# Six edits to a decoder block: pool placement, PSUM banks kept, down loads reordered, pooling sums on GpSimd, priorities, a layer norm issued later

## The chip, the cores and the metric

The kernel runs on one core of one Trainium2 chip. The metric is the device time of one execution in microseconds (us), lower is better. TensorE (PE) multiplies matrices into PSUM; VectorE (DVE), ScalarE (ACT) and GpSimd (POOL) do the rest; nearly all DMA transfers are issued by SyncE (SP).

## The reference

One decoder block over 2048 tokens of width 1024, all in float32:

```python
mod = silu(c) @ w_ada + b_ada                 # sh1, sc1, g1, sh2, sc2, g2
h = layer_norm(x) * (1 + sc1) + sh1
a_val, a_gate, u_pool, gate_a, gate_b = split(h @ w_in)    # 512, 512, 512, 1024, 1024
ya = silu(layer_norm(causal_dwconv(a_val * sigmoid(a_gate), w_dw_a))) @ w_pw_a   # 31 taps
pooled = causal_means(u_pool, windows 2, 4, 8, 16 for 128 channels each) - u_pool
yb = (pooled @ w_pool, per group) * pool_scale
mix = (sigmoid(gate_a) * ya + sigmoid(gate_b) * yb) @ w_out
x = layer_norm(ALPHA * x + g1 * mix) * ln1_g + ln1_b
h = layer_norm(x) * (1 + sc2) + sh2
v, gt = split(causal_dwconv(h @ w_up, w_dw_f))             # 3 taps, 2 x 2816 channels
x = layer_norm(ALPHA * x + g2 * ((gelu(gt) * v) @ w_down)) * ln2_g + ln2_b
```

## The kernel before

Every product runs as three matmuls on two-part operands: `split` (L203, L204) rounds a tile to a high part on ACT and takes the low part by a subtraction on DVE, or on POOL for most weights (`lo_eng`). Operands live in 128 x 512 slots: 16 of pool `hp` (name `h`), 28 of `gp` (name `g`), and later 12 named `ex`. Weight tiles are `whi` and `wlo`, 128 x 1024, in pool `ws`, four of each.

The first part runs over four passes (`q`) of 512 tokens. A pass holds: the gated products (L239 to L241) and the start of the 31-tap convolution (taps on DVE, L527); for `q` > 0 the output projection of the pass before (`project`, L488 to L490); four pooling products, each followed by the sums of a causal window; eight gate products and pool products (`evacuate`, L438, multiplies a PSUM tile by scale and gate on DVE); the norm of the convolution branch; and `merge`, which multiplies and adds into `ms` (L454, L455) and splits the result. A sum over a window of `w` tokens is made by doubling: 1, 2, 3 and 4 adds (L567) for windows of 2, 4, 8 and 16, ten in a pass, each from one buffer `us` to the next; then L570 divides and subtracts `u`, in the first pass L572 and L573 mend the first columns, and `split` gives the operands.

The kernel uses eight PSUM banks of 128 x 512. Two are `ps_tr` for transposes throughout. In the first part four are `ps_mm` and two `ps_cv` (the convolution's start); both pools belong to the stack `s1`, which is closed after the fourth pass, and a pool `ps_mm2` of six banks is opened behind it.

The last projection, `project(3, ...)`, runs behind that point, with steps of `operands` between its matmuls: these make the 28 operand tiles of the up product. Its end is the first layer norm, four row tiles: statistics, a power on POOL (L258), ACT's scaling, four DVE operations each (L506, L507) and a store to `x1_dram`. Steps of `operands` reuse slots that the projection's matmuls release.

The up product runs over two halves of 1024 tokens (`hf`), 22 units each (`u`). A unit is one step of Strassen's scheme, seven products of `multiply` (L793 to L795); the weights come from `UpWeights`, whose sums run on POOL (L714). In the first half a generator `task`, advanced at four places of a unit from the second unit on, makes the second half's operands (`h2_store`). The results go to `f_dram`. In the second half `down_operands` stores the down weights' seven combinations (`dh_...`, `dl_...`) to DRAM.

The down product (L813 to L815) runs Strassen's seven combinations (`STEPS`) over 11 k tiles, two k tiles for each pair of weight loads (L947). `Gated.fetch` (L848) loads tiles of `f`, 256 KB each; a weight load is 512 KB. In step `s3` of the first half the operand of k tile `k` is made of `f[0][k]` and `f[1][k]` by L918. The loads of k tiles 0 to 7 are issued in the last unit of the up product, those of 8 to 10 ahead of the first weights, and during `s3` two tiles of `f[1][11...]` behind each weight pair, for the next step.

The order on each engine is made by the tile framework's scheduler, which places instructions by priority (program order, unless `high_priority` or `issue_after` says otherwise) and its own estimate of times. Each engine then runs its queue in that order, waiting on semaphores. SP's queue holds loads and stores alike; in it a transfer waits for one that was issued eight transfers earlier.

## Time and profile before

| | us |
|---|---|
| median of 3 runs | 2321.76 |
| lowest and highest | 2320.23, 2323.77 |
| the profiled execution | 2322.59 |
| its span | 2320.7 |

The profile's page gives busy time by engine, the list of waits says for whom an engine stood idle and how long, a table of windows gives busy times and the granted clock of TensorE for stretches of the span, and a timeline gives instructions one after the other. Times in a timeline start with the span. A matmul's duration in a row is longer than its turn on the engine, since matmuls overlap; the pace is read from the starts, 0.23 us apart at full clock. PEclk is the granted clock as a share of the higher of its two levels (2.4 GHz; the lower is 1.2).

### The profile page before, as it was taken

Reading aid. Unit: us, or ns where it says so; the run is one execution under the profiler, and the core shown is the slowest. Engines: PE = TensorE matmul, PEld = TensorE weight load, DVE = VectorE, ACT = ScalarE, POOL = GpSimd, SP = SyncE. Lnnn points to the kernel's source line nnn. Section 1 sums busy time; section 2 is a strip of 40 time slices with the busy share of each in tenths; the row PEclk is TensorE's granted clock in tenths of the full one; section 3 lists DMA queues with packets and bytes.
Section 4 is the critical chain, followed back from the end, with each engine's and each line's share of the span. In section 5 each row is a group of like instructions: output and inputs, shape, how many; then the busy total and the mean of one; then the engine's idle time right before and its main releaser. Section 6 shows DMA issues by size and latency. Waiting matters only on the chain.

```text
span 2320.7 us, 28743 instructions
## 1 busy us (share of the span) xinstructions
PE 2246.5 (97%) x9889; PEld 1834.1 (79%) x9889; DVE 1783.0 (77%) x2769; ACT 795.4 (34%) x1213; POOL 541.5 (23%) x428
## 2 busy tenths in 40 slices
PE   5999999999999999989999999999999989999997
PEld 4777887888887888768888888888888868887885
DVE  7996779476967695798899988877777774487467
ACT  3434121321232033246555445433333332333222
POOL 0543230000110010046555564522231300000000
PEclk9999999999999999999999999999999999999998
DMA  9988877585676577779999885999999997598665
GB/s 330 346 272 295 286 266 274 200 308 199 254 294 245 189 274 262 287 259 334 341 343 349 304 321 196 345 375 339 367 345 369 363 355 267 191 355 299 243 213 195
DMA packets 293227, 675.85 MB, mean 291 GB/s; under 512 B 24249, under 2 KB 113077, under 8 KB 293082
## 3 DMA queue, kind: packets, MB, share of 16 engines
q1 hardware_dynamic: 293082, 674.02, 80.3%
q8 instruction: 78, 1.28, 0.2%
q14 instruction: 67, 0.55, 0.1%
HBM read 460.53 MB, written 213.39 MB: 290 GB/s over the span
## 4 chain that ended last, share of the span: by engine, by line
PE 88%; DVE 5%; DMA 4%; issue 1%; ACT 1%; POOL 1%; SPq 1%; DVEq 0%; POOLq 0%; ACTq 0%
PE mm L793 11%; PE mm L795 11%; PE mm L794 11%; PE mm L239 9%; PE mm L241 9%; PE mm L240 9%; PE mm L813 6%; PE mm L815 6%; PE mm L814 6%; PE mm L488 2%; PE mm L489 2%; PE mm L490 2%; PE tr L278 1%; DMA g<-in_w_ada_dram 1%; DMA raw<-in_w_ada_dram 1%
## 5 line engine op out<-in xcount | busy, mean ns | idle before, releaser
L239 PE MATMUL mm<-h,whi 128*128 128x512 f32 x896 | 354.5, 398 | 5.9 <-DVE g L438 2.3
L240 PE MATMUL mm<-h,whi 128*128 128x512 f32 x896 | 351.9, 393 | 0.2 <-DVE h L204 0.2
L241 PE MATMUL mm<-h,wlo 128*128 128x512 f32 x896 | 351.6, 393 | 0.0
L527 DVE SCALAR_TENSOR_TENSOR cv<-y,wa,cv 128x512 f32<-128x512 f32 x464 | 318.6, 749 | 3.2 <-ACT cv L519 1.8
L804 DVE SCALAR_TENSOR_TENSOR o<-mm,wf,o 128x511 f32<-128x511 f32 (+2 forms) x352 | 257.5, 743 | 39.1 <-ACT o L800 34.7
L813 PE MATMUL mm<-whi,ex 128*128 128x512 f32 x616 | 241.0, 398 | 9.4 <-DMA whi<-dh_t 9.4
L814 PE MATMUL mm<-wlo,ex 128*128 128x512 f32 x616 | 243.9, 396 | 0.0
L815 PE MATMUL mm<-whi,ex 128*128 128x512 f32 x616 | 241.6, 396 | 0.0
L204 POOL TENSOR_TENSOR wlo<-raw,whi 128x512 fp32r<-128x512 f32 (+1 forms) x109 | 197.0, 1820 | 190.9 <-ACT whi L203 143.7
L800 ACT ACTIVATE o<-mm,par,wf 128x512 f32<-128x512 f32 x176 | 136.8, 779 | 304.7 <-DVE mm L889 183.5
L793 PE MATMUL mm<-g,whi 128*128 128x512 f32 x616 | 240.4, 391 | 0.7 <-DMA g<-xh_t 0.7
L794 PE MATMUL mm<-g,whi 128*128 128x512 f32 x616 | 241.1, 391 | 0.0
L795 PE MATMUL mm<-g,wlo 128*128 128x512 f32 x616 | 235.4, 390 | 0.0
L239 PEld LDWEIGHTS mm<-h,whi 128*128 128x128 f32 x896 | 169.5, 189 | 45.1 <-DVE g L438 2.8
L240 PEld LDWEIGHTS mm<-h,whi 128*128 128x128 f32 x896 | 169.8, 190 | 36.6 <-issue 1.6
L241 PEld LDWEIGHTS mm<-h,wlo 128*128 128x128 f32 x896 | 169.3, 189 | 35.6 <-issue 0.2
L258 POOL TENSOR_TENSOR rs<-ve,mhalf 128x1 f32<-128x1 f32 x64 | 40.8, 652 | 627.3 <-DVE ve L256 460.6
L813 PEld LDWEIGHTS mm<-whi,ex 128*128 128x128 f32 x616 | 116.2, 189 | 38.1 <-ACT ex L203 9.8
L793 PE MATMUL mm<-h,whi 128*128 128x512 f32 x352 | 138.6, 394 | 3.2 <-ACT whi L203 3.2
L795 PE MATMUL mm<-h,wlo 128*128 128x512 f32 x352 | 138.4, 393 | 1.7 <-DVE wlo L204 1.7
L794 PE MATMUL mm<-h,whi 128*128 128x512 f32 x352 | 138.4, 393 | 0.0
L815 PEld LDWEIGHTS mm<-whi,ex 128*128 128x128 f32 x616 | 115.9, 188 | 28.4 <-DVE ex L204 0.4
(223 smaller groups left out, 4311.9 us busy)
## 6 DMA issues: line engine op xcount, KB each, us to landing
whi<-hi_in SPq DMA_DIRECT2D x84, 512.0 KB, 4.5
wlo<-lo_in SPq DMA_DIRECT2D x84, 512.0 KB, 4.4
uh<-whi SPq DMA_DIRECT2D x70, 512.0 KB, 4.5
ul<-wlo SPq DMA_DIRECT2D x70, 512.0 KB, 4.8
whi<-uh SPq DMA_DIRECT2D x70, 512.0 KB, 5.3
wlo<-ul SPq DMA_DIRECT2D x70, 512.0 KB, 7.8
raw<-in_w_up_dram SPq DMA_DIRECT2D x48, 512.0 KB, 7.2
f<-o SPq DMA_DIRECT2D x44, 512.0 KB, 4.5
```

The costliest lines, as they stand in the source:

```text
L204: return (lo_eng or nc.vector).tensor_sub(lo, src, hi)
L239: nc.tensor.matmul(ps, lhsT=whi[k][:, ms], rhs=xhi, start=(k == 0), stop=False)
L240: nc.tensor.matmul(ps, lhsT=whi[k][:, ms], rhs=xlo, start=False, stop=False)
L241: nc.tensor.matmul(ps, lhsT=wlo[k][:, ms], rhs=xhi, start=False, stop=(k == n - 1))
L527: nc.vector.scalar_tensor_tensor(dst, ys[j][:, k:k + T], wa[:, j, k:k + 1], o, ALU.mult, ALU.add)
L793: nc.tensor.matmul(ps, lhsT=whi[:, k, :], rhs=xhi, start=(k == 0), stop=False)
L794: nc.tensor.matmul(ps, lhsT=whi[:, k, :], rhs=xlo, start=False, stop=False)
L795: nc.tensor.matmul(ps, lhsT=wlo[:, k, :], rhs=xhi, start=False, stop=(k == len(xs) - 1))
L804: nc.vector.scalar_tensor_tensor(dst, y[:, :n], wf[:, tap, t:t + 1], dst, ALU.mult, ALU.add)
L813: nc.tensor.matmul(ps, lhsT=fhi[:, tk], rhs=whi, start=(k == 0), stop=False)
L814: nc.tensor.matmul(ps, lhsT=fhi[:, tk], rhs=wlo, start=False, stop=False)
L815: nc.tensor.matmul(ps, lhsT=flo[:, tk], rhs=whi, start=False, stop=(k == NK - 1))
```

## The change

Six edits. (1) The pools `xp` and `sm` are placed at the other end of SBUF (`side="right"`), and an unused tile `pad` with its memset goes. (2) `ps_mm` and `ps_cv` belong to the kernel's own stack and are kept after the fourth pass; `psum()` then takes banks from both by a fixed turn, two of `ps_cv`, four of `ps_mm`. (3) In the last pass the merge's operations behind a matmul, and the projection's evacuation in every pass, get high priority. (4) The pooling sums run on GpSimd. (5) The last layer norm of the first part becomes a generator, which `task` runs through ahead of `h2_store`, and `task` is advanced in the first unit as well. (6) Of the first down loads those of k tiles 0 to 4 are issued ahead of the first weights, the rest two k tiles behind each weight pair of `s3`, and from the third pair on three tiles `f[1][11...]` behind each.

```diff
-    xp = ctx.enter_context(tc.tile_pool(name="xp", bufs=5))
-    sm = ctx.enter_context(tc.tile_pool(name="sm", bufs=6))
+    xp = ctx.enter_context(tc.tile_pool(name="xp", bufs=5, side="right"))
+    sm = ctx.enter_context(tc.tile_pool(name="sm", bufs=6, side="right"))
...
-    pad = sm.tile([P, 16], F32, name="pad", tag="pad", bufs=1)
-    nc.vector.memset(pad, 0.0)
+    turns = None
     def psum():
+        if turns is not None and next(turns):
+            return ps_cv.tile([P, T], F32, name="cv", tag="cv")
         return ps_mm.tile([P, T], F32, name="mm", tag="mm")
...
-    ps_mm = s1.enter_context(tc.tile_pool(name="ps_mm", bufs=4, space=bass.MemoryType.PSUM))
-    ps_cv = s1.enter_context(tc.tile_pool(name="ps_cv", bufs=2, space=bass.MemoryType.PSUM))
+    ps_mm = ctx.enter_context(tc.tile_pool(name="ps_mm", bufs=4, space=bass.MemoryType.PSUM))
+    ps_cv = ctx.enter_context(tc.tile_pool(name="ps_cv", bufs=2, space=bass.MemoryType.PSUM))
...
-            nc.vector.tensor_mul(sga[j], pa, sga[j])
-            nc.vector.tensor_add(ms[j], ms[j], sga[j])
-            hi, lo = slot(F32R), slot(F32R)
-            split(hi, lo, ms[j])
+            with tc.high_priority() if q == NQ - 1 else nullcontext():
+                nc.vector.tensor_mul(sga[j], pa, sga[j])
+                nc.vector.tensor_add(ms[j], ms[j], sga[j])
+                hi, lo = slot(F32R), slot(F32R)
+                split(hi, lo, ms[j])
...
-            for i in range(T // P):
-                nc.vector.scalar_tensor_tensor(zs[i][:, cl], zs[i][:, cl], ALPHA, po[i], ALU.mult, ALU.add)
+            with tc.high_priority():
+                for i in range(T // P):
+                    nc.vector.scalar_tensor_tensor(zs[i][:, cl], zs[i][:, cl], ALPHA, po[i], ALU.mult, ALU.add)
...
+        def norm():
+            for i in range(T // P):
+                z = zs[i]
+                normalise(z)
...
+                nc.sync.dma_start(x1_dram[q * (T // P) + i], z)
+                yield
+        return norm()
...
-            project(q - 1, mg)
+            for _ in project(q - 1, mg):
+                pass
...
-                nc.vector.tensor_add(nxt[:, a:], cur[:, a:], cur[:, a - d:15 + T - d])
+                nc.gpsimd.tensor_add(nxt[:, a:], cur[:, a:], cur[:, a - d:15 + T - d])
...
-    ps_mm = ctx.enter_context(tc.tile_pool(name="ps_mm2", bufs=6, space=bass.MemoryType.PSUM))
+    turns = cycle((True, True, False, False, False, False))
...
-        task = chain(h2_store(2), h2_store(3)) if hf == 0 else None
+        task = chain(last_norm, h2_store(2), h2_store(3)) if hf == 0 else None
...
-                if u and name in ("x11", "t2", "t3", "t4"):
+                if name in ("x11", "t2", "t3", "t4"):
...
-                gated.fetch((0, 1), range(8))
+                gated.fetch((0, 1), range(5))
...
-        if hf == 0:
-            gated.fetch((0, 1), range(8, NK))
+        rest = iter(range(5, NK)) if hf == 0 else iter(())
+        ahead = iter(range(NK, NF))
...
-                        gated.fetch((1,), [NK + kk for kk in ks])
+                        gated.fetch((0, 1), [kk for _, kk in zip(ks, rest)])
+                        if k >= 4:
+                            gated.fetch((1,), list(islice(ahead, 3)))
```

What the scheduler makes of it is shown at three places. In these rows a line stands first, then the operation, the output, `<-` and the inputs with buffer numbers, and what the instruction waits for. Line numbers after the change are 2 to 9 higher.

The first place is DVE in the first pass, from the last taps of the pooling stretch to the first evacuation (`us` are pooling sums, `cv` the convolution). Before:

```order
L567 TENSOR_TENSOR us_999<-us_997 128x512 [waits DVE_49]
L527 SCALAR_TENSOR_TENSOR cv_586<-y_582,wa_106,cv_586 128x512 [waits DVE_49]
L527 SCALAR_TENSOR_TENSOR cv_645<-y_641,wa_106,cv_645 128x512 [waits DVE_49]
L570 SCALAR_TENSOR_TENSOR us_1001<-us_999,u_989 128x512 [waits DVE_49]
L527 SCALAR_TENSOR_TENSOR cv_586<-y_582,wa_106,cv_586 128x512 [waits DVE_49]
L527 SCALAR_TENSOR_TENSOR cv_645<-y_641,wa_106,cv_645 128x512 [waits DVE_49]
L572 TENSOR_TENSOR us_1001<-us_999,rcnt_89 128x15 [waits DVE_49]
L573 TENSOR_TENSOR us_1001<-us_1001,u_989 128x15 [waits DVE_49]
L204 TENSOR_TENSOR g_1006<-us_1001,g_1005 128x512 [waits Activation_49]
L438 SCALAR_TENSOR_TENSOR g_1186<-mm_1182,par_105,sg_1180 128x512 [waits PE_49]
```

The same stretch of DVE after the change:

```order
L535 SCALAR_TENSOR_TENSOR cv_584<-y_580,wa_104,cv_584 128x512 [waits DVE_49]
L535 SCALAR_TENSOR_TENSOR cv_643<-y_639,wa_104,cv_643 128x512 [waits DVE_49]
L579 SCALAR_TENSOR_TENSOR us_999<-us_997,u_987 128x512 [waits Pool_49]
L581 TENSOR_TENSOR us_999<-us_997,rcnt_87 128x15 [waits DVE_49]
L582 TENSOR_TENSOR us_999<-us_999,u_987 128x15 [waits DVE_49]
L206 TENSOR_TENSOR g_1004<-us_999,g_1003 128x512 [waits Activation_49]
L440 SCALAR_TENSOR_TENSOR g_1184<-mm_1180,par_103,sg_1178 128x512 [waits PE_49]
```

And POOL there after the change, with the last four adds (`wlo` are weights):

```order
L206 TENSOR_TENSOR wlo_1231<-raw_1232,whi_1230 128x1024 [waits DMAHW3_49,DMAHW7_49,PE_49,Activation_49]
L570 COPY uh_798<-u_987 128x15 [waits Activation_49]
L576 TENSOR_TENSOR us_991<-u_987 128x526 [waits Pool_49]
L568 COPY u_2885<-uh_798 128x15 [waits DVE_49]
L576 TENSOR_TENSOR us_993<-us_991 128x524 [waits Pool_49]
L206 TENSOR_TENSOR wlo_1274<-raw_1275,whi_1273 128x1024 [waits DMAHW5_49,DMAHW6_49,PE_49,Activation_49]
L576 TENSOR_TENSOR us_995<-us_993 128x520 [waits DVE_49,Pool_49]
L576 TENSOR_TENSOR us_997<-us_995 128x512 [waits Pool_49]
L206 TENSOR_TENSOR wlo_1317<-raw_1318,whi_1316 128x1024 [waits DMAHW0_49,DMAHW1_49,PE_49,Activation_49]
```

The adds left DVE and stand between POOL's weight subtractions; the last subtraction of the pooling (L570, now L579) waits for POOL, the taps between it and L573 have moved ahead, and the evacuation L438 (now L440) follows it directly.

The second place is TensorE from the last merge product (L239 to L241) to the last projection's first matmuls. Before:

```order
L241 MATMUL mm_7846<-g_7631,wlo_7824 128x512
L488 MATMUL mm_7884<-whi_7888,g_7716 128x512 [waits DMAHW4_49,DVE_49,Activation_49]
L489 MATMUL mm_7884<-wlo_7889,g_7716 128x512 [waits DMAHW5_49]
L490 MATMUL mm_7884<-whi_7888,g_7717 128x512
L488 MATMUL mm_7885<-whi_7888,g_7716 128x512
```

After:

```order
L243 MATMUL mm_7844<-g_7629,wlo_7822 128x512
L491 MATMUL cv_7877<-whi_7881,g_7714 128x512 [waits DMAHW4_49,Activation_49]
L492 MATMUL cv_7877<-wlo_7882,g_7714 128x512 [waits DMAHW5_49]
L493 MATMUL cv_7877<-whi_7881,g_7715 128x512
L491 MATMUL cv_7878<-whi_7881,g_7714 128x512
L492 MATMUL cv_7878<-wlo_7882,g_7714 128x512
L493 MATMUL cv_7878<-whi_7881,g_7715 128x512
L491 MATMUL mm_7879<-whi_7881,g_7714 128x512 [waits DVE_49]
```

The first two accumulators are banks of `ps_cv` now, without a wait for DVE; the third and fourth are banks of `ps_mm` and wait for DVE.

The third place is SP's queue at the start of the down product (`h` and `g` are tiles of `f`, `dh_t3` and `dl_t3` the stored weights). Before, with four loads of `f` left out of the print ahead of it:

```order
L848 DMA h_16062<-f0_4_8388 128x512 [waits DMAHW7_49,PE_49]
L848 DMA h_16063<-f0_5_8389 128x512 [waits DMAHW0_49,PE_49]
L848 DMA h_16064<-f0_5_8389 128x512 [waits DMAHW1_49,PE_49]
L848 DMA h_16065<-f0_6_8390 128x512 [waits DMAHW2_49,PE_49]
L848 DMA h_16066<-f0_6_8390 128x512 [waits DMAHW3_49,PE_49]
L848 DMA h_16067<-f0_7_8391 128x512 [waits DMAHW4_49,PE_49]
L848 DMA h_16068<-f0_7_8391 128x512 [waits DMAHW5_49,PE_49]
```

Then come six loads of `f` for the k tiles 8 to 10, and behind them:

```order
L947 DMA whi_16202<-dh_t3_8436 128x1024 [waits DMAHW4_49]
L947 DMA wlo_16203<-dl_t3_8437 128x1024 [waits DMAHW5_49]
L848 DMA g_16206<-f0_11_8395 128x512 [waits DMAHW6_49,PE_49]
L848 DMA g_16207<-f0_12_8396 128x512 [waits DMAHW7_49,PE_49]
L947 DMA whi_16246<-dh_t3_8436 128x1024 [waits DMAHW0_49]
```

After:

```order
L857 DMA h_16055<-f0_4_8317 128x512 [waits DMAHW7_49,PE_49]
L956 DMA whi_16171<-dh_t3_8365 128x1024 [waits DMAHW0_49]
L956 DMA wlo_16172<-dl_t3_8366 128x1024 [waits DMAHW1_49]
L857 DMA h_16175<-f0_5_8318 128x512 [waits DMAHW2_49,PE_49]
L857 DMA h_16176<-f0_5_8318 128x512 [waits DMAHW3_49,PE_49]
L857 DMA h_16177<-f0_6_8319 128x512 [waits DMAHW4_49,PE_49]
L857 DMA h_16178<-f0_6_8319 128x512 [waits DMAHW5_49,PE_49]
L956 DMA whi_16219<-dh_t3_8365 128x1024 [waits DMAHW6_49,PE_49]
L956 DMA wlo_16220<-dl_t3_8366 128x1024 [waits DMAHW7_49,PE_49]
```

The first weight pair follows ten loads of `f` instead of 22, and four more loads stand between it and the second pair. Between the second and third pair stand four loads as well; between the third and the fourth four loads, three stores of weights of the last `down_operands`, and three loads of `f[1][11...]`; between the fourth and fifth one such store, three loads and the store of the last unit's result (512 KB).

## Rows read from the trace of the kernel before

**Rows 1.** Page, busy us, share of the span and instructions of each engine.

```profile
PE 2246.5 (97%) x9889; PEld 1834.1 (79%) x9889; DVE 1783.0 (77%) x2769; ACT 795.4 (34%) x1213; POOL 541.5 (23%) x428
```

**Rows 2.** TensorE's waits: line, releaser, us in total, times, longest.

```profile
PE mm L813 <- DMA whi<-dh_t: 9.4, 1, 9.4
...
PE mm L239 <- DVE g L438: 5.7, 2, 3.3
...
PE mm L488 <- ACT g L203: 3.7, 1, 3.7
...
PE mm L793 <- ACT ht L878: 2.6, 1, 2.6
PE mm L795 <- DVE wlo L204: 2.2, 2, 1.7
```

**Rows 3.** Windows: length, PE, PEld, DVE, ACT, POOL busy, PEclk, DMA share, GB/s.

```profile
120.00:136.00 16.00, 13.65 (x54) 10.82 (x54) 15.28 (x24) 4.75 (x7) 6.55 (x4) 0.89 0.84 280
945.00:957.00 12.00, 8.31 (x31) 6.49 (x30) 11.78 (x20) 4.81 (x8) 0.00 (x0) 0.86 0.85 320
960.00:990.00 30.00, 30.00 (x134) 24.86 (x133) 15.23 (x24) 4.07 (x7) 0.00 (x0) 1.00 0.65 234
```

**Rows 4.** Timelines, first pass: start, us, engine, line, operation, [idle before <-releaser].

```profile
110.49 2.51 POOL L204 TENSOR_TENSOR wlo<-raw,whi 128x1024 fp32r<-128x1024 f32 x1 [1.46 <-ACT whi L203]
...
110.66 1.41 DVE L527 SCALAR_TENSOR_TENSOR cv<-y,wa,cv 128x512 f32<-128x512 f32 x2
111.97 1.58 DVE L570 SCALAR_TENSOR_TENSOR us<-us,u 128x512 f32<-128x512 f32 x1
...
117.51 1.05 ACT L203 CAST whi<-raw 128x1024 fp32r<-128x1024 f32 x1
...
125.97 0.18 DVE L573 TENSOR_TENSOR us<-us,u 128x15 f32<-128x15 f32 x1
126.83 0.69 DVE L204 TENSOR_TENSOR g<-us,g 128x512 fp32r<-128x512 f32 x1 [0.68 <-ACT g L203]
127.44 0.74 DVE L438 SCALAR_TENSOR_TENSOR g<-mm,par,sg 128x512 f32<-128x512 f32 x1
...
128.23 0.80 PE L239 MATMUL mm<-h,whi 128*128 128x512 f32 x1 [2.35 <-DVE g L438]
```

**Rows 5.** Lines L567, L714: count, ns min/median/max, first and last start.

```profile
L567 DVE TENSOR_TENSOR us<-us x24: 636/680/2574, 103.4 to 843.4; 128x512 f32<-128x512 f32 x12, 128x516 f32<-128x516 f32 x4, 128x524 f32<-128x524 f32 x4, 128x520 f32<-128x520 f32 x4
L567 DVE TENSOR_TENSOR us<-u x16: 681/692/2496, 91.9 to 836.6; 128x512 f32<-128x512 f32 x4, 128x514 f32<-128x514 f32 x4, 128x518 f32<-128x518 f32 x4, 128x526 f32<-128x526 f32 x4
...
L714 POOL TENSOR_TENSOR st<-raw x24: 1284/1300/2361, 1000.0 to 1453.6; 128x512 f32<-128x512 f32 x24
```

**Rows 6.** Timelines, second pass: POOL, DVE and TensorE.

```profile
337.98 10.37 POOL L561 COPY uh<-u 128x15 f32<-128x15 f32 x2 [2.21 <-ACT u L560]
...
376.59 1.28 DVE L179 SCALAR_TENSOR_TENSOR xt<-raw,silu_c,xt 128x1024 f32<-128x1024 f32 x1 [0.34 <-DMA raw<-in_w_ada_dram]
...
378.40 2.06 DVE L438 SCALAR_TENSOR_TENSOR g<-mm,par,sg 128x512 f32<-128x512 f32 x3
...
379.19 0.50 PE L239 MATMUL mm<-g,whi 128*128 128x512 f32 x1 [3.35 <-DVE g L438]
```

**Rows 7.** Timelines, DVE and TensorE at the start of the last projection.

```profile
950.26 0.69 DVE L454 TENSOR_TENSOR g<-mm,g 128x512 f32<-128x512 f32 x1
...
951.05 0.77 PE L488 MATMUL mm<-whi,g 128*128 128x512 f32 x1 [3.69 <-ACT g L203]
```

**Rows 8.** Timelines, SP and TensorE at the down start, and a window behind it.

```profile
1856.73 4.45 SPq L848 DMA_DIRECT2D h<-f  x7
...
1866.00 0.32 SPq L947 DMA_DIRECT2D whi<-dh_t  x1
...
1872.11 2.05 PE L813 MATMUL mm<-whi,ex 128*128 128x512 f32 x4 [9.39 <-DMA whi<-dh_t]
...
1880.00:1890.00 10.00, 10.00 (x44) 8.04 (x44) 6.86 (x11) 1.38 (x3) 0.00 (x0) 1.00 1.04 412
```

More of the change, by code (lines that the diff above doesn't have):

```diff
@@ L1 @@
-from contextlib import ExitStack
-from itertools import chain
+from contextlib import ExitStack, nullcontext
+from itertools import chain, cycle, islice
 import concourse.bass as bass
@@ L500, in project @@
                 nc.sync.dma_start(gb[2 * i + hh], v[:, hh * T:(hh + 1) * T].broadcast_to([P, T]))
-        for i in range(T // P):
-            z = zs[i]
-            normalise(z)
-            for hh in range(2):
-                cl = slice(hh * T, (hh + 1) * T)
-                nc.vector.tensor_mul(z[:, cl], z[:, cl], gb[hh])
-                nc.vector.tensor_add(z[:, cl], z[:, cl], gb[2 + hh])
-            nc.sync.dma_start(x1_dram[q * (T // P) + i], z)
+        def norm():
+            for i in range(T // P):
+                z = zs[i]
+                normalise(z)
+                for hh in range(2):
+                    cl = slice(hh * T, (hh + 1) * T)
+                    nc.vector.tensor_mul(z[:, cl], z[:, cl], gb[hh])
+                    nc.vector.tensor_add(z[:, cl], z[:, cl], gb[2 + hh])
+                nc.sync.dma_start(x1_dram[q * (T // P) + i], z)
+                yield
+        return norm()
     yh = uh = None
@@ L692, in decoder_block @@
     gb = [t[:, hh * T:(hh + 1) * T] for t in (otile(), otile()) for hh in range(2)]
-    project(NQ - 1, mg, gb, {(0, 0): 1, (0, 1): 1, (0, 2): 1, (0, 3): 1, (0, 4): 1, (0, 5): 1, (0, 6): 1, (0, 7): 1,
+    last_norm = project(NQ - 1, mg, gb, {(0, 0): 1, (0, 1): 1, (0, 2): 1, (0, 3): 1, (0, 4): 1, (0, 5): 1, (0, 6): 1, (0, 7): 1,
                              (1, 0): 1, (1, 2): 1, (1, 5): 1, (1, 7): 1})
```

## Prediction

> **What bounds the kernel now.** I read the page's line of busy times, then TensorE's waits, then the stretches in which the larger waits lie. TensorE is busy for 2246.5 us of a span of 2320.7 us [rows 1], so only about 74 us of its time are idle, and no other engine's total matters by itself: an edit is worth what it takes out of these 74 us, plus what the clock loses behind a stall. The list of waits [rows 2] names five single events that the change touches: 9.4 us before the first matmul of the down product (a load of `whi`), 2.35 + 3.35 us before matmuls that wait for the evacuation at L438, 3.7 us at the start of the last output projection (L488), and 2.6 and 1.7 us in the first unit of the up product. The other events it leaves alone. The windows around the events [rows 3] show the second price: after a stop of 2.35 us and more the granted clock stands at the lower of its two levels for a few us. Over the 16 us around 128 us the mean is 0.89, which is 0.11 x 16 = 1.8 us lost; 0.14 x 12 = 1.7 us around 951 us. At 379 and 1872 us, behind stops as long or longer, I charge the same, 1.8 and 1.7 us. So the events cost: 128 us, 2.35 + 1.8 = 4.1; 379 us, 3.35 + 1.8 = 5.1; 951 us, 3.7 + 1.7 = 5.4; 1872 us, 9.4 + 1.7 = 11.1. Together 25.7 us are within reach.
>
> **Pooling sums on GpSimd.** DVE loses 40 adds of about 0.68 us, ten in each of the four passes [rows 5], and POOL gains them. A POOL operation of the same kind and size (L714) has a median of 1.30 us and a longest of 2.36 us [rows 5]; I take 1.30, the median beside ordinary load. What it is worth is read where DVE is late.
>
> First pass. TensorE was ready at 128.23 - 2.35 = 125.88 us, and DVE began L438 only at 127.44 us [rows 4]; DVE was busy for 15.28 of 16 us there [rows 3], so its work set the time. Afterwards L438 (L440 by its new number) stands right behind the last pooling subtraction, which waits for POOL's last add, and POOL has the weight subtraction (`wlo_1274`) ahead of the last two adds. That subtraction waits for ACT's cast, which ran at 117.51 to 118.56 us [rows 4]. If the cast stays there: 118.56 + 2.5 (the POOL subtraction [rows 4]) + 2 x 1.30 = 123.7; the subtraction on DVE takes 0.7 like an add, and from the start of the two edge operations to L438 it was 1.7 us (the second began at 125.97, L438 at 127.44 [rows 4], with one of 0.2 ahead): L440 starts at 126.1 instead of 127.44. TensorE then waits 2.35 - 1.3 = 1.05 us, too short to lower the clock, I assume: gain 1.3 + 1.8 = 3.1. If the cast comes earlier, since the cast queued ahead of it on ACT waits for DVE's pooling work, nothing is left: gain 4.1. With adds of 1.8 us that follow each other the end is 5 us later: a loss of about 1. I take 3.2, near the first, bounds -1 and 4.1.
>
> Second pass. TensorE was ready at 379.19 - 3.35 = 375.84; L438 began at 378.40 [rows 6]. Ten adds of 0.68 leave DVE ahead of it, 6.8 us, and it now stands before four of the five `w_ada` steps (1.28 us, the last of them right ahead of it [rows 6]) that ran first: 5.1 more, 11.9 in all, so that POOL sets the time. Its chain begins when DVE's block of layer norm operations ends, at 348 (the copies at 337.98 end there [rows 6]): ten adds at 1.30 are 13 us, four subtractions between them that wait and are waited for 3, small POOL work 2, and the way from the last subtraction to L440, 4: 370, 5 us early. Gain 5.1; with adds of 1.8 us still early. Bounds 1 and 5.1.
>
> Third and fourth pass. No stall stands there now, so nothing is gained; 20 adds on POOL stand ahead of the small POOL operations of the layer norms and of DVE's evacuations. I charge 1 us, bounds 0 and 6.
>
> One row speaks against the edit. While POOL ran a subtraction with two SBUF inputs from 110.49 for 2.51 us, two convolution taps, which read PSUM and one SBUF tile, took their usual 0.7 us each, but the next operation with two SBUF inputs took 1.58 us: it stood until POOL was done [rows 4]. The Trainium skill, "SBUF — State Buffer", section "Who interferes with whom", says that such a DVE instruction contends with a GpSimd one that reads SBUF, and that the later of them is blocked for all of the other's run; the trace agrees. I keep my sum, since the DVE work next to the adds is mostly taps; the other case is a rival below.
>
> **PSUM banks kept.** At 947 us the merge matmuls are over; the first projection matmul starts at 951.05. The profile names ACT, but the row of the order also waits for DVE, since the new pool's banks start where all old ones end, and DVE read the last merge bank (L454) from 950.26 to 950.95 [rows 7]. Afterwards the first two accumulators are the two `ps_cv` banks and wait for no DVE; the third and fourth, 6 x 0.23 = 1.4 us later, wait for merge steps 4 and 5, the third and fourth from the end, which is early enough. Gain 5.4, bounds 3 and 5.4. What is late next is the up weights' chain; it follows TensorE's own release of operand slots and DVE is busy for 15.2 of the 30 us from 960 on [rows 3], so I let it move along. Setting the merge (and L496) ahead of other work costs DVE nothing: the same instructions.
>
> **Down loads in another order.** Now 22 loads of `f` stand in SP's queue before the first weights, which go out at 1866.00 and are used at 1872.11, 6.1 us later; TensorE was ready at 1862.7 [rows 8]. Afterwards the pair stands behind ten, two rows behind the point that SP reached at 1856.73 [rows 8]; SP's issues are 0.7 us apart there (seven in 4.45 us), so it goes out at about 1857.4 and 1858.1. With 6.1 us, and 0.3 for what is still under way ahead of it, first use is at 1863.8: a stop of 1.1 us. But the queue is full: the DMA engines are busy all through, at 412 GB/s from 1880 to 1890 [rows 8], and at 400 a load of 256 KB takes 0.65 us. A pair of k tiles takes TensorE 24 matmuls, 5.5 us by 44 in 10 us [rows 8]; 5.6 allows for records missing. Between the first and second, and second and third weight pairs, SP's order holds 2 MB, 5.2 us: TensorE is fed. Between the third and the fourth there are four `f` loads, three stores and three early `f` loads beside the weights, 14 x 0.65 = 9.1 us: data at 1863.8 + 5.2 + 5.2 + 9.1 = 1883.3, TensorE ready at 1863.8 + 3 x 5.6 = 1880.6, a stop of 2.7 us and 1.7 us of lowered clock. The fifth pair comes 12 x 0.65 = 7.8 us on, at 1891.1, against 1883.3 + 5.6 + 1.7 = 1890.6: 0.5. In all 1.1 + 2.7 + 1.7 + 0.5 = 6.0 in place of 11.1: gain 5.1. Bounds: 10 (nothing late afterwards) and 1 (all paid back; the loads are the same bytes).
>
> **Layer norm put off, and pools.** The norm's instructions are issued in the first unit now, but on DVE the sixteen multiplies and adds stand where they stood, ahead of the first unit's later weight splits; the stalls of 2.6 and 1.7 us [rows 2] stay: 0, between a loss of 2 and a gain of 4. The pools at SBUF's other end change addresses alone, and the removed memset is under 1 us of DVE at the start, which no row of the waits names: 0.
>
> **Sum.** 3.2 + 5.1 - 1.0 + 5.4 + 5.1 + 0 = 17.8 us. The profiled execution took 2322.6 us, 0.8 us above the median of the runs, 2321.8. From the median: 2304.0.
>
> **Rivals.**
> *The down start pays nothing back.* If the early `f` loads are late enough to let the fourth weights pass, the gain there is 10 and the time 2304.0 - 4.9 = 2299. For it: before, TensorE ran from 1880 on without a stop beside saturated DMA [rows 8]. Against: the fourth pair then followed fewer loads. 14%.
> *The down start pays all back.* 2304.0 + 4.1 = 2308. The same bytes must come in over one saturated stretch. 12%.
> *POOL takes back what DVE gave.* Each add on POOL can hold one DVE operation with two SBUF inputs until it ends, up to 1.30 us, as the subtraction held one for 0.9 us [rows 4]: 40 x 1.30 = 52 us at most, against 40 x 0.68 = 27 us that DVE is relieved of [rows 5]. Then L438 (L440) comes as late as before in both passes: 2304.0 + 3.2 + 5.1 = 2312. Against: the taps aren't held, and the second pass has 5 us of room. 13%. The rule of the Trainium skill named above ("SBUF — State Buffer", "Who interferes with whom") is this case.
> *Adds starve on POOL, and the kernel gets slower.* In the second pass two copies of 15 columns stood on POOL for 10.37 us [rows 6], beside DVE's block of layer norm operations with two SBUF inputs. If each add takes 2.5 us instead of 1.3, the chain ends 8 us later in the first pass and 12 us in the others; with 5 us of room in the last three, TensorE stands for 9 + 7 + 7 + 7 us and the clock adds 4 x 1.8, 37 us against the 9.2 that these places cost now: 28 us worse there, 10.5 better elsewhere, 2339. The sign turns from adds of about 2.0 us on: 7 x 0.7 + 1.8 us in the first pass and 3 x (10 x 0.7 - 5 + 1.8) in the others are 18 us, the whole sum. The block lies ahead of most of the adds, so: 6%.
> *The relief is passed on.* The up weights' chain or SP's queue is late by what TensorE gained; of the 17.8 us some 3 stay: 2319. 5%.
>
> **How the numbers follow.** My forecast has 50%, by itself 2300 to 2308. Eight in ten lie between 2297 and 2314: above stand the starving adds, the relief passed on and part of the POOL chain; below, a part of the full down gain. A measurement of this kernel tells about 0.2%, 4.6 us, from no change. Faster by more: 0.50 + 0.14 + 0.12 + 0.13 = 0.89; within: the relief passed on, 0.05; slower: the starving adds, 0.06.
>
> **What would show it.** Right: TensorE's waits no longer list L438 (L440) with more than 1 us, L488 (L491) starts within 0.5 us of the last merge matmul, the first L813 (L822) waits under 2 us and a stop of 1 to 4 us stands three pairs later; the POOL adds have a median near 1.3 us. Wrong: adds with a median over 1.8 us, a wait behind L579, a clock that is lowered where it wasn't, or new waits between 990 and 1040 us.

## The result, and the profile after

The changed kernel takes 2296.66 us (median of 4 runs, 2294.50 to 2299.18); the kernel before, beside it, 2322.77 (4 runs, 2320.23 to 2327.92). The ratio is 0.9885, with a 95% interval of 0.9863 to 0.9907: 26 us faster, where 17.8 were forecast. The time lies 0.3 us below the range of 2297 to 2314. Its sign was right; a mechanism that the prediction had put at nothing was the largest of all.

The page's line of busy times, of the kernel after:

```profile
PE 2228.4 (97%) x9889; PEld 1831.1 (80%) x9889; DVE 1768.4 (77%) x2728; ACT 794.3 (35%) x1213; POOL 587.6 (26%) x468
```

This line holds the surprise. The span is 2296.8 us in place of 2320.7, 23.9 less. TensorE is idle for 2296.8 - 2228.4 = 68.4 us in place of 74.2 [rows 1]: 5.8 us of the 23.9. The other 18.1 us are **busy time** that TensorE has lost while it ran the same 9889 matmuls. The whole prediction was about idle time.

TensorE's waits in the kernel after (line, what was waited for, us in total, times, the longest):

```profile
PE mm L822 <- DMA whi<-dh_t: 5.3, 4, 2.4
...
PE mm L802 <- ACT whi L205: 4.2, 3, 3.4
...
PE mm L491 <- DVE xt L500: 3.9, 1, 3.9
PE mm L241 <- DVE y L438: 3.4, 1, 3.4
...
PE mm L804 <- DVE wlo L206: 2.4, 4, 1.0
PE cv L822 <- ACT fh L815: 2.2, 1, 2.2
PE mm L802 <- ACT ht L887: 1.9, 1, 1.9
```

Against [rows 2], the 9.4 us before the down product (L813, now L822) have become 5.3 in four pieces, L488 (now L491) no longer waits for its PSUM bank, and the wait for `g` of L438 (now L440) is gone from the list. New are 3.9 us at L491 for `xt` and 2.2 at L822 for `fh`; the wait for `y` (L239, now L241) has grown from 1.7 to 3.4.

The stretches of [rows 3], after (columns as there):

```profile
120.00:136.00 16.00, 16.00 (x73) 13.23 (x72) 14.50 (x22) 6.79 (x9) 8.86 (x6) 1.00 0.84 279
945.00:957.00 12.00, 12.00 (x55) 9.94 (x54) 9.52 (x15) 3.71 (x6) 0.00 (x0) 1.00 0.97 353
960.00:990.00 30.00, 30.00 (x134) 24.82 (x133) 20.32 (x33) 5.96 (x10) 0.00 (x0) 1.00 0.57 194
```

The events at 128 and 951 us are gone, and the granted clock, which stood at 0.89 and 0.86 there, is at its upper level throughout.

Now the busy time. Two stretches in the middle of the down product, in which TensorE waits for nothing and the granted clock is 1.00, before:

```profile
1920.00:1960.00 40.00, 40.00 (x173) 32.21 (x172) 15.21 (x23) 11.46 (x19) 0.00 (x0) 1.00 0.79 275
2000.00:2040.00 40.00, 40.00 (x173) 32.21 (x172) 23.86 (x36) 11.46 (x19) 0.00 (x0) 1.00 0.61 205
```

and after:

```profile
1920.00:1960.00 40.00, 40.00 (x178) 33.10 (x177) 17.52 (x28) 9.07 (x16) 0.00 (x0) 1.00 0.82 301
2000.00:2040.00 40.00, 40.00 (x178) 33.10 (x178) 32.37 (x56) 16.42 (x24) 2.50 (x4) 1.00 0.82 291
```

In the same 40 us the window counts 178 matmuls in place of 173: 0.225 us each in place of 0.231. (The count takes in the matmuls that straddle an end of the window, so the true paces are about 2 ns longer.) The trace gives them better, as the mean distance of a matmul's start from the start of the one before it, over the distances of 0.2 to 0.3 us. Divided by what the second of the two reads, before and after, this gives: products on `h` 227.1 and 227.0 ns (3595 distances before), products on `g` outside the projection 228.1 and 227.0 (2266), up products on `ex` 231.4 and 226.9 (774), the down product, all of it on `ex`, 233.4 and 226.8 (1837). So it is the `ex` tiles that became quicker to multiply: 1837 x 6.6 + 774 x 4.5 + 2266 x 1.1 ns = 12.1 + 3.5 + 2.5 = 18.1 us, the 18.1 us of busy time. (The `g` products stand mixed with those on `ex` in the up product.)

The other 6 us are idle time and lowered clock. Summed up as distances between starts over the usual one, TensorE lost, in us:

| stretch | before | after |
|---|---|---|
| 60 to 80 (wait for `y`, L438) | 2.3 | 5.4 |
| 120 to 140 (first pass, L438/L440) | 4.1 | 0 |
| 300 to 320 (first projection, L488/L491) | 1.4 | 6.6 |
| 360 to 400 (second pass, L438/L440) | 5.6 | 0 |
| 940 to 960 (change of stage) | 5.3 | 0 |
| 980 to 1060 (first up unit) | 13.4 | 12.7 |
| 1240 to 1340 (later up units) | 1.3 | 3.7 |
| 1840 to 1900 (start of the down product) | 11.2 | 8.7 |
| 2060 to 2100 (second half of the down product) | 0 | 3.2 |

The four places that the prediction went for (the lines of 120, 360, 940 and 1840 us) gave 17.5 us; the others took some 13 of them back, so that little more than 4 us of the 6 stand in these lines.

### The profile page after: what moved, and what is told of

It reads as the page before. It is cut to its first block, busy times and chain, and to the rows that moved or that the text cites. A ratio compares the mean times of both kernels' runs of the same rounds, so it can differ in the third digit from the quotient of the medians.

```text
span 2296.8 us, 28699 instructions
## 1 busy us (share of the span) xinstructions
PE 2228.4 (97%) x9889; PEld 1831.1 (80%) x9889; DVE 1768.4 (77%) x2728; ACT 794.3 (35%) x1213; POOL 587.6 (26%) x468
## 4 chain that ended last, share of the span: by engine, by line
PE 81%; DVE 8%; DMA 7%; issue 2%; POOL 1%; ACT 1%; SPq 1%; DVEq 0%; POOLq 0%; ACTq 0%
PE mm L241 10%; PE mm L242 10%; PE mm L243 10%; PE mm L804 6%; PE mm L802 6%; PE mm L803 6%; PE mm L824 3%; PE mm L822 3%; PE mm L823 3%; PE cv L804 3%; PE cv L803 3%; PE cv L802 3%; PE mm L491 2%; PE mm L492 2%; PE mm L493 2%; PE cv L822 2%
## 5 line engine op out<-in xcount | busy, mean ns | idle before, releaser
L241 PE MATMUL mm<-h,whi 128*128 128x512 f32 x896 | 352.0, 395 | 5.4 <-DVE y L438 3.4
L242 PE MATMUL mm<-h,whi 128*128 128x512 f32 x896 | 351.0, 392 | 0.2 <-DVE h L206 0.2
L243 PE MATMUL mm<-h,wlo 128*128 128x512 f32 x896 | 350.9, 392 | 0.0
L241 PEld LDWEIGHTS mm<-h,whi 128*128 128x128 f32 x896 | 168.9, 189 | 43.7 <-issue 5.6
L813 DVE SCALAR_TENSOR_TENSOR o<-mm,wf,o 128x511 f32<-128x511 f32 (+2 forms) x232 | 170.3, 743 | 25.0 <-ACT o L809 23.7
L822 PE MATMUL mm<-whi,ex 128*128 128x512 f32 x418 | 161.8, 391 | 6.0 <-DMA whi<-dh_t 5.3
L823 PE MATMUL mm<-wlo,ex 128*128 128x512 f32 x418 | 163.3, 391 | 0.0
L824 PE MATMUL mm<-whi,ex 128*128 128x512 f32 x418 | 160.8, 391 | 0.1
L802 PE MATMUL mm<-g,whi 128*128 128x512 f32 x407 | 158.9, 391 | 0.0
L803 PE MATMUL mm<-g,whi 128*128 128x512 f32 x407 | 158.9, 390 | 0.0
L804 PE MATMUL mm<-g,wlo 128*128 128x512 f32 x407 | 155.3, 390 | 0.0
L205 ACT CAST whi<-raw 128x512 fp32r<-128x512 f32 (+1 forms) x137 | 98.6, 749 | 101.5 <-PE mm L242 31.9
L266 ACT ACTIVATE xt<-xt,rs 128x1024 f32<-128x1024 f32 x49 | 59.0, 1239 | 135.7 <-DVE rs L265 135.7
L813 DVE SCALAR_TENSOR_TENSOR o<-cv,wf,o 128x512 f32<-128x512 f32 (+1 forms) x120 | 88.5, 744 | 13.1 <-ACT o L809 12.2
```

Source lines behind the costliest of these rows:

```text
L241: nc.tensor.matmul(ps, lhsT=whi[k][:, ms], rhs=xhi, start=(k == 0), stop=False)
L242: nc.tensor.matmul(ps, lhsT=whi[k][:, ms], rhs=xlo, start=False, stop=False)
L243: nc.tensor.matmul(ps, lhsT=wlo[k][:, ms], rhs=xhi, start=False, stop=(k == n - 1))
L802: nc.tensor.matmul(ps, lhsT=whi[:, k, :], rhs=xhi, start=(k == 0), stop=False)
L803: nc.tensor.matmul(ps, lhsT=whi[:, k, :], rhs=xlo, start=False, stop=False)
L804: nc.tensor.matmul(ps, lhsT=wlo[:, k, :], rhs=xhi, start=False, stop=(k == len(xs) - 1))
```

## The experiments

Edit (1) does nothing but move tiles and drop a memset, so the addresses were looked up in the two programs. Each `ex` tile has rows of 2048 bytes in every partition. Before, the `ex` tiles begin at byte 198912 and end at 223488, on multiples of 256; after, at 170880 and 195456, 128 bytes beyond a multiple of 256. Their partners in a matmul, `whi` and `wlo`, and the tiles `h` and `g`, lie 128 beyond in both kernels. Three theories stood: **A**, the upper end of SBUF is slower to read; **B**, the place relative to a multiple of 256 bytes counts, either the tile's own (**B1**) or the difference between the two operands of a matmul (**B2**); **C**, the pace comes from the PSUM banks of edit (2). The forecast's own view was that edit (1) is worth nothing.

**Edit (1) alone.** To the kernel before, the first lines of the change's diff alone, down to the line that takes out the memset of `pad`.

> The kernel before with the first edit alone: pools xp and sm at SBUF's other end, the unused tile pad gone. By it the operand tiles ex move from bytes 198912 to 223488 of each partition to 170880 to 195456. Theory A (TensorE is slower on operands that lie in the upper end of SBUF): all matmuls that read ex start 0.227 us apart instead of 0.231 to 0.237; 1848 in the down product and some 780 in the up product by 5 to 7 ns make 16 us: about 2306, ratio 0.993. Theory C (the pace changed because accumulators come from two PSUM pools): the pace on ex stays at 0.233 and the time at 2322. The forecast on record said 0 for this edit.

Measured: 2305.76 us (4 runs) against 2323.29, ratio 0.9917 (0.9884 to 0.9949). The first of the two stretches above:

```profile
1920.00:1960.00 40.00, 40.00 (x178) 33.10 (x178) 18.03 (x28) 11.33 (x19) 0.00 (x0) 1.00 0.87 312
```

178 matmuls, with the PSUM pools of before: C falls. An edit that changes no matmul's work is worth 17.5 us by medians (12 to 27 by the interval), as much as the forecast gave to the other five.

**The unused tile 128 bytes wider.** To the kernel before, so that `ex` lies 128 bytes higher, at its old end of SBUF:

```diff
-    pad = sm.tile([P, 16], F32, name="pad", tag="pad", bufs=1)
+    pad = sm.tile([P, 48], F32, name="pad", tag="pad", bufs=1)
```

> The kernel before with the unused tile pad 128 bytes wider. The ex tiles then start at 199040, which is 128 bytes beyond a multiple of 256, as all other operand tiles (h, g, whi, wlo) do and as ex does in the changed kernel; before, ex started at a multiple of 256. Theory B (the alignment makes the pace): the pace on ex is 0.227 and the time about 2306. Theory A (the place in SBUF makes it): 0.233 as before, 2322.

Measured: 2311.41 us (1 run).

```profile
1920.00:1960.00 40.00, 40.00 (x179) 33.11 (x178) 15.37 (x23) 10.87 (x18) 0.00 (x0) 1.00 0.83 297
```

The fast pace at the upper end of SBUF: A falls. Of the expected gain a part went into stops elsewhere: this run's trace lost 3.4 us more than that of before at 60 to 80 us, and 5.2 more at 300 to 320.

**`ex` lower, on multiples of 256.** To the kernel before, one use more of the pool of `ex` tiles ahead of the first operands, after which `ex` lies at 182528 to 207104:

```diff
+    nc.vector.memset(extra().bitcast(F32), 0.0)
```

> The kernel before with ex allocated ahead of o in their pool (one memset of a tile of ex added). The twelve ex tiles then lie at 182528 to 207104, at multiples of 256 as before. Theory A with a border between 195456 and 198912: the tiles in the lower part run at 0.227, those in the upper part at 0.233, within one run, so the down product has about half of the slow pace and the time is some 6 to 8 us shorter, 2314 to 2316. Theory B: all at 0.233, 2322.

Measured: 2322.93 us (1 run).

```profile
1920.00:1960.00 40.00, 40.00 (x173) 32.20 (x172) 14.94 (x23) 11.46 (x19) 0.00 (x0) 1.00 0.78 274
```

173 again, some 16 KB lower: A falls a second time, from the other side.

**Everything 128 bytes on.** To the kernel before, an unused tile at the start of SBUF, by which `h`, `g`, `whi` and `wlo` come to lie on multiples of 256 and `ex` 128 beyond. B1 expects `ex` fast, and `h` and `g` slow; B2, `ex` slow as before.

```diff
+    off = const.tile([P, 32], F32, name="off", tag="off")
+    nc.vector.memset(off, 0.0)
```

> The kernel before with 128 unused bytes at the start of SBUF, so that every tile lies 128 bytes higher: h, g, whi and wlo start at multiples of 256 bytes now and ex 128 beyond one, the other way round than before. Theory B1 (a tile that starts at a multiple of 256 is slower for TensorE by itself): the matmuls on h, g, whi run at about 0.232, some 7000 of them by 5 ns, 2350 or more. Theory B2 (what counts is that the two operands of a matmul lie at different distances from a multiple of 256): as before, 0.227 without ex and 0.231 to 0.236 with it, 2322.

Measured: 2319.68 us (1 run); `h` 227.1 and `g` 228.1 ns, as before; up on `ex` 231.4, down 232.8.

```profile
1920.00:1960.00 40.00, 40.00 (x173) 32.41 (x172) 14.75 (x22) 10.23 (x17) 0.00 (x0) 1.00 0.84 299
```

`ex` now has the alignment that was fast, and is slow; `h` and `g` have the one that was slow, and are fast. B1 falls, B2 stands.

**Other differences.** To the kernel before, `pad` with 32 elements, so that `ex` and its partners differ by 64 bytes (first diff); and with 112, so that they differ by a whole 256 (second).

```diff
-    pad = sm.tile([P, 16], F32, name="pad", tag="pad", bufs=1)
+    pad = sm.tile([P, 32], F32, name="pad", tag="pad", bufs=1)
```

```diff
-    pad = sm.tile([P, 16], F32, name="pad", tag="pad", bufs=1)
+    pad = sm.tile([P, 112], F32, name="pad", tag="pad", bufs=1)
```

> The kernel before with the unused tile pad 64 bytes wider, so that ex starts 64 bytes beyond a multiple of 256 and the other operands 128 beyond one. Theory B2 (any difference counts): the pace on ex stays near 0.233, 2322. If only the distance of 128 bytes counts: 0.227, about 2307.

> The kernel before with the unused tile pad 384 bytes wider: ex starts 128 bytes beyond a multiple of 256, as the other operands do, but not at the same distance from a multiple of 512 (128 against 384). If distances are counted within 256 bytes, the pace on ex is 0.227, as with 128 bytes more; if within 512 or more, it stays slower, 0.229 to 0.236.

Measured: with 64 bytes 2321.41 us (1 run), up on `ex` 232.6 and down 228.9 ns; with 256, 2303.64 us (1 run), 226.9 and 226.7. The stretch at 1920 us with 64 bytes:

```profile
1920.00:1960.00 40.00, 40.00 (x177) 32.81 (x176) 15.44 (x23) 11.46 (x19) 0.00 (x0) 1.00 0.70 245
```

and with 256:

```profile
1920.00:1960.00 40.00, 40.00 (x178) 33.14 (x177) 18.29 (x28) 10.87 (x18) 0.00 (x0) 1.00 0.89 323
```

A whole 256 bytes of difference counts as none. At 64 the up product is as slow as at 128, and the down product only a third as much slowed; the single time, hardly below that of before, doesn't follow the 7 us of this pace (774 x 1.2 ns lost, 1837 x 4.5 won), since its profiled run lost 3.0 us more than before at 60 to 80 us, 1.1 at the start of the down product, and 0.7 and 0.8 at 940 and 2080.

The kernels that ran once decide by their paces, means of hundreds of distances, and not by their times. One thing they leave open: in each of them `h`, `g`, `whi` and `wlo` lie at one distance from a multiple of 256, and `ex` lies at the other together with the tiles `o` and `st` of its pool, so that no run moved `ex` against its matmul partner alone. But the accesses of DVE, ACT and POOL are not what slows TensorE: while they all stand idle, the down product runs at 233.3 ns before (397 distances) and at 226.7 after (370), as it does beside their work.

**The change without edit (1).** To the changed kernel, the lines of edit (1) taken back.

> The changed kernel with the first edit undone (pools and pad as before). Theory A: the pace on ex goes back to 0.231 to 0.237 and the time is 14 to 16 us longer than the changed kernel, 2311 to 2313, which is 10 us shorter than the kernel before, ratio 0.9955. Theory C: 2297, ratio 0.9885.

Measured: 2307.57 us (4 runs), ratio to before 0.9928 (0.9899 to 0.9957), 15.7 us by medians; pace on `ex` 231.3 (up) and 232.4 ns (down).

```profile
1920.00:1960.00 40.00, 40.00 (x174) 32.43 (x173) 17.93 (x29) 9.41 (x16) 0.00 (x0) 1.00 0.81 289
```

The other five edits together are worth what the forecast gave them, 17.8, within the interval (10 to 23 us). Above the whole change this kernel is by 10.9 us, while its slower `ex` should cost 1837 x 5.6 + 774 x 4.4 + 2266 x 1.3 ns = 16.6. Its profiled run lost 2.0 and 1.5 us at the stops of 65 and 308 us where that of the whole change lost 5.4 and 6.6, which would leave 8.1; the measured 10.9 lies between the two.

**Pooling sums on GpSimd alone** (edit 4, the one line with `tensor_add` in the change's diff).

> The kernel before with the fourth edit alone, the pooling sums on GpSimd. By the prediction the waits for the evacuation near 128 and 379 us go, 9.2 us, with nothing lost elsewhere by this edit: 2313, ratio 0.996. Rival (the relief is passed on): what TensorE gains at 128 us it stands again near 308 us, where the last weights of the first projection are scaled on DVE at the pace of their loads, and the time is 2317 to 2319, ratio 0.998.

Measured: 2313.73 us (9 runs) against 2324.70, ratio 0.9952 (0.9939 to 0.9965): 11 us. The stretches of the first and of the second pass:

```profile
120.00:136.00 16.00, 16.00 (x72) 13.27 (x71) 14.50 (x22) 6.78 (x9) 8.88 (x7) 1.00 0.81 263
...
372.00:388.00 16.00, 15.97 (x71) 12.90 (x70) 16.00 (x26) 4.17 (x5) 1.53 (x3) 1.00 0.81 279
```

Both stops are gone, by this edit alone, with the clock's fall behind each. The rival's place, near 308 us, did grow in the profiled run:

```profile
310.36 0.77 PE L488 MATMUL mm<-whi,g 128*128 128x512 f32 x1 [3.92 <-DVE xt L496]
```

With the slower clock behind it this stop cost 6.7 us in place of 1.4. That run took 2319.85 us, the longest of the nine; the median lies below the 2317 to 2319 that the rival gave.

**PSUM banks alone** (edit 2, without the priorities of edit 3).

> The kernel before with the second edit alone (PSUM pools kept, banks taken by turns), without the priorities. By the prediction the wait at the start of the last projection (3.7 us and 1.7 us of lowered clock) goes and nothing else changes: 2318, ratio 0.9977. Rival (the relief is passed on to the up weights' chain): the stop moves to the stretch from 980 to 1040 us, 2322. The pace on ex stays at 0.233.

Measured: 2321.82 us (10 runs) against 2323.71, ratio 0.9990 (0.9978 to 1.0001).

```profile
945.00:957.00 12.00, 12.00 (x55) 9.94 (x54) 11.62 (x21) 4.75 (x8) 0.00 (x0) 1.00 0.89 333
```

The stop at 951 us is gone, but the time shows at most 5 us of it and by its medians 2; the interval reaches to no change at all. The profiled run has new waits in the up units:

```profile
1035.98 0.50 PE L797 MATMUL mm<-g,whi 128*128 128x512 f32 x1 [1.29 <-ACT fh L810]
...
1329.28 0.50 PE L797 MATMUL cv<-h,whi 128*128 128x512 f32 x1 [1.17 <-ACT whi L207]
```

The first is for a bank that ACT has not read out (`fh`), which came by the turn. The second stands in the middle of a product and is for a weight tile that ACT cast late, no bank. Another 3.9 us stand in the first projection, for `xt`. The pace on `ex` is 231.4 and 232.4 ns: C falls once more.

**Down loads alone** (edit 6).

> The kernel before with the sixth edit alone (order of the first down loads). By the prediction the first stop falls from 9.4 to about 1.1 us, a stop of about 2.5 us appears three weight pairs later, and the sum is 5 us less: 2318, ratio 0.9978. In the changed kernel a wait of 2.2 us for a bank of the last up unit stood at the fourth accumulator: if it comes with the load order (the 9.4 us hid it), it stands here too and the gain is 3; if it comes with the PSUM turns, it doesn't.

Measured: 2319.95 us (10 runs), ratio 0.9992 (0.9978 to 1.0007): 3.8 us by medians, not clear of noise. TensorE at the start of the down product, in order of time, rows with a wait alone:

```profile
1861.95 0.94 PE L813 MATMUL mm<-whi,ex 128*128 128x512 f32 x3 [1.27 <-DMA whi<-dh_t]
...
1864.91 0.50 PE L813 MATMUL mm<-whi,ex 128*128 128x512 f32 x1 [2.02 <-ACT fh L806]
...
1883.77 1.17 PE L813 MATMUL mm<-whi,ex 128*128 128x512 f32 x4 [0.94 <-DMA whi<-dh_t]
...
1891.81 0.47 PE L813 MATMUL mm<-whi,ex 128*128 128x512 f32 x1 [1.97 <-DMA whi<-dh_t]
```

The single stop of 9.4 us is now four, 6.2 us in all. The second is for a PSUM bank: the down product's fourth accumulator takes a bank that the last up unit has not handed over (`fh`, L806). It comes with the load order alone, without the PSUM turns, so the 9.4 us had covered it.

**Layer norm put off, alone** (edit 5).

> The kernel before with the fifth edit alone (last layer norm issued inside the first up unit). By the prediction it changes nothing, between 2 us longer and 4 us shorter: 2320, ratio 0.999; stops of 13 us in all from 980 to 1040 us, as before.

Measured: 2322.64 us (10 runs), ratio 0.9994 (0.9984 to 1.0005): nothing, as forecast.

**Other banks at two places.** To the changed kernel: the third and fourth accumulators of the first down group, and two of the first projection's, take banks of the pool that serves the transposes.

```diff
-            po = [psum() for _ in range(T // P)]
+            po = [psum_tr() if q == 0 and hh and i < 2 else psum() for i in range(T // P)]
...
-            po = [psum() for _ in range(T // P)]
+            po = [psum_tr() if hf == 0 and a == "s3" and i > 1 else psum() for i in range(T // P)]
```

> The changed kernel with two new edits against its own new waits: the third and fourth accumulators of the first down step use the two transpose banks, which are idle there (a wait of 2.2 us for ACT's copy from an up product's bank stands at the fourth now), and the first two accumulators of the second half of the first projection use them as well (a wait of 3.9 us for DVE's evacuation and a lowered clock of 1.7 us stand there now). If these waits are what they seem, 4 to 7 us less than the changed kernel: 2290 to 2293, ratio 0.986. If something else is late at the same places (the load of weights at the down start, the weights' scaling at 308 us), 2295 to 2297.

Measured: 2293.65 us (4 runs), ratio to before 0.9864 (0.9841 to 0.9886). The waits at the start of its down product:

```profile
1849.98 0.70 PE L822 MATMUL mm<-whi,ex 128*128 128x512 f32 x2 [2.29 <-DMA whi<-dh_t]
...
1870.45 0.70 PE L822 MATMUL mm<-whi,ex 128*128 128x512 f32 x2 [1.92 <-DMA whi<-dh_t]
```

The wait for `fh` and the stop at 308 us are gone; 3 us are left of them by medians (5 by the two ratios), and the interval overlaps that of the changed kernel, so that it is not shown to be the faster. At the start of the down product the free banks gave nothing: from 1840 to 1900 us this run lost 8.8 us and that of the changed kernel 8.7, since TensorE came to the loads 3 us earlier and waited longer for them.

Edit (3), the priorities, was not run alone.

## Why the prediction was wrong, point by point

**The step that failed** is the sentence "The pools at SBUF's other end change addresses alone … 0". Addresses alone were worth 17.5 us (12 to 27), more than any term of the sum. A matmul whose two operands lie at different distances from a multiple of 256 bytes took 1 to 3% longer here, and edit (1) brings `ex` to the distance of `whi` and `wlo`. It could have been read beforehand, not as a cause but as a doubt: 40 us by 173 matmuls is 0.231 us in the down product (the stretch at 1920 us above), against 30 us by 134 in the last projection [rows 3], 0.224. The prediction took its pace from 44 matmuls in 10 us [rows 8], too short a stretch to tell 0.225 from 0.231, and the 5.6 us that it allowed for 24 matmuls, 0.233 each, it put down to "records missing". Had it set 0.231 against 0.224 for the 2611 matmuls on `ex`, 18 us, as the far end of what moved addresses may give, the range would have held the result.

**The other terms** came near their sum, and that is in part luck. By medians the edits run alone gave 11.0 (edit 4), 1.9 (edit 2), 3.8 (edit 6) and 1.1 us (edit 5), 17.7 beside the 17.8 forecast; but one term was too small and two were too large, and the intervals of the last three reach to no change at all.

**Pooling sums, first pass**: 3.2 forecast, 4.1 gained in the profiled runs, the upper bound. DVE and POOL there, after:

```profile
122.19 0.69 DVE L579 SCALAR_TENSOR_TENSOR us<-us,u 128x512 f32<-128x512 f32 x1 [0.74 <-POOL us L576]
122.92 2.25 DVE L581 TENSOR_TENSOR us<-us,rcnt 128x15 f32<-128x15 f32 x1
...
126.68 1.40 DVE L440 SCALAR_TENSOR_TENSOR g<-mm,par,sg 128x512 f32<-128x512 f32 x2
```

```profile
119.71 2.45 POOL L576 TENSOR_TENSOR us<-us 128x520 f32<-128x520 f32 x2
122.36 2.78 POOL L206 TENSOR_TENSOR wlo<-raw,whi 128x1024 fp32r<-128x1024 f32 x1 [0.20 <-ACT whi L205]
```

ACT's cast came earlier, so the weight subtraction stood ahead of the last two adds and the next one behind them. DVE waited 0.74 us for POOL (L579), the rival's wait, and L440 began at 126.68, where 126.1 was forecast and 127.44 was before [rows 4]. In between an operation on 15 columns took 2.25 us and ended as POOL's subtraction did (at 125.17 and 125.14): the hold that the prediction had read from [rows 4], in a second place. The Trainium skill states such a hold ("SBUF — State Buffer", "Who interferes with whom"), and the trace agrees. On DVE the sum was 0.6 us too early. That TensorE doesn't wait at all is luck: it is 3.1 us later than before by the stop at 65 us. In the change without edit (1), which lost less at 65, a stop of 1.18 us stands here, with the clock kept; 1.05 was forecast.

**The adds on POOL** (duration in ns: least, median, longest):

```profile
L576 POOL TENSOR_TENSOR us<-us x24: 1036/1058/1373, 103.4 to 832.3; 128x512 f32<-128x512 f32 x12, 128x516 f32<-128x516 f32 x4, 128x524 f32<-128x524 f32 x4, 128x520 f32<-128x520 f32 x4
...
L576 POOL TENSOR_TENSOR us<-u x16: 1037/1052/1533, 94.3 to 827.2; 128x512 f32<-128x512 f32 x4, 128x514 f32<-128x514 f32 x4, 128x518 f32<-128x518 f32 x4, 128x526 f32<-128x526 f32 x4
```

1.06 us where 1.30 was taken from L714, and none over 1.53. The starving adds (2.0 us and more) never came, and "POOL takes back" held single operations without reaching TensorE. **Second pass**: 5.1 forecast, 5.6 gained in the profiled runs. **Third and fourth pass**: the 1 us charged is not seen; no wait stands there. Edit (4) alone gave 11 us (8 to 14) where these terms had 7.3. The two stops are not steady by themselves: in the ten profiled runs whose sums stay on DVE they cost 4.7 to 10.2 us together, 7.3 in the mean, and in the four with the sums on POOL at most 1.5.

**PSUM banks**: 5.4 forecast, and the row at 951 us gives it: no stop is left there. As a whole edit (2) alone gave 0 to 5, so the term was right at its place and wrong as a total: that run has a new wait of 1.29 us for a bank, and its stops at 65 and 308 us, which are no effect of the banks as far as the runs show, were 2.7 and 5.1 us longer than before.

**Down loads**: 5.1 forecast, 2.5 gained. TensorE there, rows with a wait alone:

```profile
1851.78 0.70 PE L822 MATMUL mm<-whi,ex 128*128 128x512 f32 x2 [1.07 <-DMA whi<-dh_t]
...
1854.95 0.50 PE L822 MATMUL cv<-whi,ex 128*128 128x512 f32 x1 [2.24 <-ACT fh L815]
...
1873.31 0.81 PE L822 MATMUL mm<-whi,ex 128*128 128x512 f32 x2 [2.42 <-DMA whi<-dh_t]
...
1880.94 0.47 PE L822 MATMUL mm<-whi,ex 128*128 128x512 f32 x1 [0.32 <-DMA whi<-dh_t]
```

The three stops for loads were forecast as 1.1, 2.7 and 0.5 and measured 1.07, 2.42 and 0.32, with the clock's 1.6 behind the second (0.96 over the 40 us from 1860 on). What stands beside them is the bank wait of 2.24 us, which the 9.4 us had covered. It is not the whole of what was missed: with the transpose banks, where this wait is gone, the stops for loads were 2.29 and 1.92 us, the clock fell behind each of them, and the stretch cost as much as with it. So the agreement of the three stops is in part luck, and as far as these two runs show the loads bound this stretch with and without the bank. Two more stops, 1.46 us for weights and 0.72 for `ex`, came at 2070 and 2093 us, where before TensorE ran through beside 402 GB/s. The quicker pace alone doesn't explain them: the change without edit (1), at the slow pace, lost 1.9 us there, and edit (1) alone 1.8.

**Layer norm**: 0 forecast, 0 measured. The first up unit lost 13.4 us before and 12.7 after.

**The longer stops at 65 and 308 us** were in no term. They take back 8.3 us in the profiled run of after:

```profile
308.75 0.77 PE L491 MATMUL mm<-whi,g 128*128 128x512 f32 x1 [3.92 <-DVE xt L500]
```

They are no effect of one edit: the stop at 308 us costs 1.4 to 1.9 us in nine of the profiled runs and 6.5 to 6.8 in four, and among these four is the kernel whose unused tile is 128 bytes wider, whose instructions are those of before. What decides between them stays open; no experiment here set it off alone. By medians, edit (1) alone (17.5) and the other five (15.7) make 33 us where the whole has 26; these stops and the loads at 2070 us are where a part of the difference stands, but the intervals of the two are too wide (12 to 27, and 10 to 23) to say that anything is missing.

## What to carry to other kernels

Divide a full stretch by its matmuls in each stage: when one tile's matmuls run at another pace than the others', with the same shape and the clock granted, look at that tile's address against its partner's before putting it down to missing records. A change that moves pools or drops a pad is then a change to TensorE's pace. And when the longest stop is shortened, ask what else waits in the same stretch: here a PSUM bank's wait of 2.2 us came up from under a load, and with the bank free the loads took its place.

## What the runs showed of the hardware

A matmul of these kernels with 512 columns ran at about 0.227 us when its two operands lay at the same distance from a multiple of 256 bytes in their partitions (`h` with `whi` both 128 beyond or both on it, `ex` with `whi` both 128 beyond, by multiples of 512 too or not). When they differed by 64 it took 0.229 us in the down product and 0.233 in the up product, and when they differed by 128, 0.232 to 0.233 and 0.231 (means of some 1830 and 780 distances). The place in SBUF and each operand's own alignment didn't matter. The means hide a pattern: in the down product of the kernel before, the distances alternate between about 229 and 238 ns over long stretches, where they are 226 or 227 after the change. Differences below 64 and of other sizes weren't tried, and why it is so no run here shows.
